# Seven block products for eight in the gate and up projections of a hybrid decoder step

## The chip, the cores and the metric

The kernel runs on one core of a Trainium2 chip. The metric is the device time of one execution in microseconds (us). The core has a matrix engine (TensorE, PE in the profile), a vector engine (VectorE, DVE), a scalar engine (ScalarE, ACT), a general engine (GpSimd, POOL) and a queue that issues the transfers (SyncE, SP).

## The reference

One layer is computed for 520 tokens, 512 of a prompt and 8 of a sample group, in float32:

```
x = x + 0.5 * swiglu(rmsnorm(x, n1), gate1, up1, down1)
h = rmsnorm(x, nm);  p = h @ w_in
     group A: x/B/C through a causal conv of width 4 and SiLU, state-space scan
              (16 heads x 64, state 128, chunks of 256), times SiLU(z), grouped norm
     group B: y = Bg * conv_w3(Cg * h_in)            (1024 channels)
x = x + concat(A, B) @ w_out
x = x + 0.5 * swiglu(rmsnorm(x, n2), gate2, up2, down2);  y = rmsnorm(x, nf)
swiglu(x) = (silu(x @ w_gate) * (x @ w_up)) @ w_down
```

The model width is 1024 (8 tiles of 128 channels), the hidden width of a half step 2816 (22 tiles), the joint projection `w_in` has 45 tiles of columns. Final states of the scan and of both convolutions are outputs too.

## The kernel before, in words

Activations lie with channels on the partitions and 520 tokens along the free axis. Every large product is made of *weight units*: up to 8 k-tiles of 128 output columns (512 KB). A unit is loaded on the SP queue and split into two parts in a reduced format whose sum is the float32 weight: ScalarE casts `hi` (L91), VectorE subtracts to get `lo` (L92). The activations are split in the same way (`xh`, `xl`). A k-tile then takes three terms, hi with xh, hi with xl and lo with xh, each for two halves of 260 tokens: six matmuls of 128x260 (`mm_k`, L118), 48 a unit. `unit` keeps one unit split ahead; `whl` has three buffers.

The stages: (1) loads of x, with the first two units cut into pieces so that products follow the loads, and GpSimd summing the squares for the norm. (2) The first half step, `ffn`: 22 times a gate unit and an up unit of 48 matmuls; VectorE takes the gate's result times the norm factor r out of PSUM (L283), ScalarE applies SiLU (L284), VectorE multiplies by r and by the up result (L285, L287) and the hidden tile is split (L290, L291). Behind all 22, the way down: 8 output tiles of 22 k-tiles (132 matmuls), each added to x by one pass (L299) and handed to `after`, which prepares the next norm. (3) The mixer: the `dt` unit, 12 conv tiles, then 24 products of the short conv during which the scan and the sample group are advanced piece by piece (`pump`), then the gate `z`, the grouped norm and the 16 units of `w_out`. (4) The second half step; its last output tile goes by token halves, each followed by the final norm of that half (`last`).

A norm factor (`factor`, L168 to L170) is a product with ones over the summed squares, a square root on ScalarE and a reciprocal on VectorE. The order of instructions on each engine comes from a scheduler that works by priorities, from the order of the code, and from estimated times; `high_priority` moves a piece forward. Tiles of one tag rotate through the buffers of their pool; a pool opened after another has closed may lie in its memory.

Of the kernel before, what the change touches and what calls it, by code (L numbers as in the profile page):

```python
# [16 lines left out]
P = 128  # L17
D = 1024
KD = D // P                  # k-tiles of the model width
SEQ = 512  # L20
NB = 8                       # sample sequences, one new token each
T = SEQ + NB                 # all tokens, prompt first
H2 = T // 2                  # tokens of one matmul
FF = 2816
KF = FF // P
NH = 16                      # SSD heads of 64 channels
HD = 64
NG = 2                       # B/C groups
NS = 128                     # state size
CW = 4                       # conv widths  # L30
SW = 3
NX = 12                      # tiles of x, B, C
NCH = SEQ // P               # blocks of 128 positions
NC2 = NCH // 2               # scan chunks of two blocks
EPS = 1e-6
KU = 8                       # k-tiles of one weight unit
WARM = 8                     # products that bring the tensor engine's clock up

# packed per-channel parameters: name -> (first column, columns)
# [15 lines left out]
def of(t):  # L55
    """k-tile k of a tile [128, k, tokens]"""
    return lambda k: t[:, k]
# [5 lines left out]

class Core:
    """The pieces that every phase uses: weight units, products, norm factors."""

    def __init__(self, nc, tc, ctx, a, order):
# [5 lines left out]
        self.wst = pool("wst", 2)  # L73
        self.whl = pool("whl", 3)
        self.nrm = pool("nrm", 2)
        self.xp = pool("xp", 1)
        self.mm = pool("mm", 3, space=space.PSUM)
        self.aux = pool("aux", 2, space=space.PSUM)
        self.dram = pool("dram", 1, space=space.DRAM)
        self.order, self.at, self.ready = order, 0, []  # L80

    # a weight unit: up to 8 k-tiles of 128 output columns, split into two float32r
    # parts whose sum is the float32 weight
    def parts(self):
        hi = self.whl.tile([P, KU, P], F32R, tag="hi", name="hi")
        lo = self.whl.tile([P, KU, P], F32R, tag="lo", name="lo")
        return hi, lo

    def split_w(self, src, st, hi, lo):
        self.nc.sync.dma_start(st, src)  # L90
        self.S.copy(hi, st)  # L91
        self.V.tensor_tensor(lo, st, hi.bitcast(F32), op=ALU.subtract)  # L92

    def fetch(self):
        if self.at == len(self.order):
            return
        src, nk, *dt = self.order[self.at]
        self.at += 1
        st = self.wst.tile([P, KU, P], F32, tag="st", name="st")
        hi, lo = self.parts()  # L100
        if any(dt):  # both parts of the few dt weights in one stationary operand
            self.nc.sync.dma_start(st, src)
            s = slice(2 * NH, 3 * NH)
            self.S.copy(hi, st)
            self.V.tensor_tensor(hi[:, :, s], st[:, :, s], hi[:, :, s].bitcast(F32), op=ALU.subtract)
        else:
            self.split_w(src, st[:, :nk], hi[:, :nk], lo[:, :nk])
        self.ready.append((hi, lo, nk))

    def unit(self, ahead=1):  # L110
        while len(self.ready) < 1 + ahead and self.at < len(self.order):
            self.fetch()
        return self.ready.pop(0)

    def mm_k(self, ps, hi, lo, k, xh, xl, first, last, hs=(0, 1)):
        for n, (w, x) in enumerate(((hi, xh), (hi, xl), (lo, xh))):
            for h in hs:
# [3 lines left out]
    def mm_unit(self, ps, u, xh, xl, first=True, last=True, hs=(0, 1)):  # L121
        hi, lo, nk = u
        for k in range(nk):
            self.mm_k(ps, hi, lo, k, xh(k), xl(k), first and k == 0, last and k == nk - 1, hs)
# [663 lines left out]
```

## Time and profile before

| | us |
|---|---|
| three runs | 1194.73, 1196.69, 1198.38 |
| median | 1196.69 |
| span of the profiled execution | 1193.0 |

For the profiled execution the span from its first to its last instruction is what is listed; the median of the runs stands 3.7 us above it, which is taken as what lies around the span. [...] Matmuls are pipelined, so the duration of one (0.28 us) is its latency; the distance between their starts is what a product costs.

### The profile page before, as it was taken

The numbers are of one execution on the slowest core, as the hardware profiler recorded it, in microseconds if no ns is written. First come the engines' busy times: TensorE is split into PE (matmuls) and PEld (weight loads), VectorE is DVE, ScalarE is ACT, GpSimd is POOL, SyncE is SP. The second block draws the span as 40 slices with busy tenths as digits, with TensorE's granted clock in tenths as the row PEclk, the third lists the DMA queues.
The fourth block names the chain that finished last, engine by engine and source line by source line (L and its number), as shares of the span: only waits on it lengthen the run. The fifth ranks groups of instructions, "written<-read, shape, count | busy, mean of one in ns | idle before, by whom it ended". The sixth has DMA issues, their size and how long they took to land.

```text
span 1193.0 us, 22147 instructions
## 1 busy us (share of the span) xinstructions
PE 1163.1 (97%) x9583; PEld 1150.2 (96%) x9583; DVE 632.9 (53%) x810; ACT 384.1 (32%) x524; POOL 254.0 (21%) x318
## 2 busy tenths in 40 slices
PE   8999999999999999998899999999999999999996
PEld 7999999999999999987889999999999999999996
DVE  7544444443333678889987476445444444432224
ACT  5322222222222466344332343223222222222221
POOL 4000000000222377567643232320000000001112
PEclk8999999999999999999999999999999999999998
DMA  5322222222332432455533222222222222232322
GB/s 197 101 96 89 89 89 92 101 87 80 98 95 89 123 107 95 144 186 166 187 107 95 78 89 91 103 90 90 89 89 92 100 93 89 90 97 81 98 81 72
DMA packets 50361, 122.99 MB, mean 103 GB/s; under 512 B 9880, under 2 KB 19256, under 8 KB 50264
## 3 DMA queue, kind: packets, MB, share of 16 engines
q1 hardware_dynamic: 50264, 121.58, 31.4%
q8 instruction: 75, 1.23, 0.4%
q14 instruction: 22, 0.18, 0.0%
HBM read 114.43 MB, written 7.14 MB: 102 GB/s over the span
## 4 chain that ended last, share of the span: by engine, by line
PE 87%; POOL 4%; DVE 4%; issue 2%; DMA 2%; ACT 1%; SPq 0%; DVEq 0%; POOLq 0%; ACTq 0%
PE mmt L118 85%; POOL st L623 1%; POOL up L622 1%; DMA out_ss<-st 1%; DMA x<-in_xT 1%; DVE lo L92 1%; DMA st<-in_ssm 1%; DVE s L561 0%; POOL t L654 0%; POOL t L653 0%; DVE s L541 0%; PE auxt L168 0%; PE mmt L403 0%; POOL xd L616 0%; DVE up L625 0%
## 5 line engine op out<-in xcount | busy, mean ns | idle before, releaser
L118 PE MATMUL mmt<-xh,hi 128*128 128x260 f32 x2112 | 429.3, 284 | 1.7 <-ACT xh L178 1.7
L118 PE MATMUL mmt<-xh,lo 128*128 128x260 f32 x2112 | 426.8, 284 | 1.0 <-DVE lo L92 1.0
L118 PE MATMUL mmt<-xl,hi 128*128 128x260 f32 x2112 | 426.8, 284 | 0.8 <-DVE xl L179 0.7
L91 ACT CAST hi<-st 128x1024 fp32r<-128x1024 f32 (+2 forms) x202 | 202.6, 1005 | 644.0 <-issue 361.7
L92 DVE TENSOR_TENSOR lo<-st,hi 128x1024 fp32r<-128x1024 f32 (+2 forms) x202 | 245.2, 1215 | 177.9 <-ACT hi L91 176.7
L118 PEld LDWEIGHTS mmt<-xh,hi 128*128 128x128 f32 x2112 | 327.1, 189 | 2.8 <-ACT xh L178 1.9
L118 PEld LDWEIGHTS mmt<-xh,lo 128*128 128x128 f32 x2112 | 326.6, 189 | 1.8 <-DVE lo L92 1.6
L118 PEld LDWEIGHTS mmt<-xl,hi 128*128 128x128 f32 x2112 | 325.8, 189 | 1.6 <-DVE xl L179 1.5
L118 PE MATMUL mmt<-hh,hi 128*128 128x260 f32 x704 | 146.5, 285 | 0.0
L118 PE MATMUL mmt<-hh,lo 128*128 128x260 f32 x704 | 145.7, 283 | 0.0
L118 PE MATMUL mmt<-hl,hi 128*128 128x260 f32 x704 | 144.5, 281 | 0.0
L143 POOL TENSOR_TENSOR acc<-x 128x520 f32<-128x520 f32 x4 | 5.4, 1349 | 560.2 <-DVE x L299 538.0
L118 PEld LDWEIGHTS mmt<-hl,hi 128*128 128x128 f32 x704 | 110.6, 189 | 0.0
L118 PEld LDWEIGHTS mmt<-hh,hi 128*128 128x128 f32 x704 | 110.5, 189 | 0.1
L118 PEld LDWEIGHTS mmt<-hh,lo 128*128 128x128 f32 x704 | 109.3, 188 | 0.0
L287 DVE TENSOR_TENSOR h<-mmt,g 128x520 f32<-128x520 f32 x44 | 30.8, 700 | 124.3 <-PE mmt L118 124.2
L283 DVE TENSOR_TENSOR g<-mmt,r 128x520 f32<-128x520 f32 x44 | 30.8, 699 | 122.9 <-PE mmt L118 122.9
L146 POOL TENSOR_TENSOR sq<-x 128x520 f32<-128x520 f32 x22 | 35.4, 1609 | 196.6 <-DVE x L299 129.8
L147 POOL TENSOR_TENSOR acc<-acc,sq 128x520 f32<-128x520 f32 x28 | 43.8, 1563 | 2.2
L179 DVE SCALAR_TENSOR_TENSOR xl<-x,pc,xh 128x520 fp32r<-128x520 f32 (+1 forms) x25 | 32.8, 1323 | 4.8 <-ACT xh L178 4.8
L285 DVE TENSOR_TENSOR g<-g,r 128x520 f32<-128x520 f32 x44 | 30.4, 694 | 1.4 <-ACT g L284 1.4
L291 DVE TENSOR_TENSOR hl<-h,hh 128x520 fp32r<-128x520 f32 x44 | 30.5, 694 | 0.7 <-ACT hh L290 0.7
(193 smaller groups left out, 1015.2 us busy)
## 6 DMA issues: line engine op xcount, KB each, us to landing
st<-in_wi SPq DMA_DIRECT2D x45, 512.0 KB, 3.5
st<-in_wg SPq DMA_DIRECT2D x43, 512.0 KB, 3.5
st<-in_wu SPq DMA_DIRECT2D x43, 512.0 KB, 3.4
st<-in_wd SPq DMA_DIRECT2D x32, 512.0 KB, 3.4
st<-in_wo SPq DMA_DIRECT2D x16, 512.0 KB, 3.6
st<-in_wd SPq DMA_DIRECT2D x16, 384.0 KB, 3.1
st<-in_ssm SPq DMA_DIRECT2D x16, 256.0 KB, 2.8
s<-scr SPq DMA_DIRECT2D x8, 512.0 KB, 4.7
```

The costliest lines, as they stand in the source:

```text
L91: self.S.copy(hi, st)
L92: self.V.tensor_tensor(lo, st, hi.bitcast(F32), op=ALU.subtract)
L118: self.PE.matmul(ps[:, h, :H2], w[:, k, :], x[:, h * H2:(h + 1) * H2], start=first and n == 0, stop=last and n == 2)
L146: eng.tensor_tensor(sq, xt, xt, op=ALU.mult)
L147: eng.tensor_tensor(acc, acc, sq, op=ALU.add)
L179: self.V.scalar_tensor_tensor(xl, xt, w, xh.bitcast(F32), op0=ALU.mult, op1=ALU.subtract)
L283: V.tensor_tensor(halves(g), pg[:, :, :H2], halves(r), op=ALU.mult)
L285: V.tensor_tensor(g, g, r, op=ALU.mult)
L287: V.tensor_tensor(halves(hf), pu[:, :, :H2], halves(g), op=ALU.mult)
L291: V.tensor_tensor(b_, hf, a_.bitcast(F32), op=ALU.subtract)
L622: G.tensor_tensor(up, bb, xd.unsqueeze(2).broadcast_to([P, HB, NS]), op=ALU.mult)
L623: G.tensor_tensor(st, st, up, op=ALU.add)
```

## The change

Gate and up no longer run as units of 128 columns but as 11 *groups* of 256 columns each. A group is a product of 2x2 blocks (columns in two tiles, tokens in two halves, channels in pairs of tiles), done with seven block products where the plain way has eight, in Winograd's form. The weights of a group come in one tile of four blocks (1 MB, `_blocks`); `adds` makes the sums of the weight blocks on VectorE, `split` splits a block pair at a time, four steps a group, four steps ahead of use (`whl` has four buffers). The activation side is made once a half step by `variants`, seven versions of 260 tokens for each pair of channel tiles. `group` accumulates the seven blocks in three PSUM banks X, Z and Y; X is read by ScalarE three times in between (`keep`), and VectorE combines the outputs (`put`, `c12`). The mixer keeps plain products (`Plain`).

The way down stays plain but is cut into four chunks of hidden pairs (`CH`), whose units are laid between later groups (`steps`), two, one, two, one and two at a time; x takes a VectorE pass of 260 tokens for each unit and half. At the end the last two output tiles go together by token halves. The squares for the norms of later stages are made by ScalarE, GpSimd only sums. In the mixer the short conv's result stays whole (`yt`) and is split into `ch` and `cl` in the gate stage. The first loads are the tiles of x, with the first weight group behind the first two. PSUM for a half step is six banks for groups and two for the rest.

```diff
-        self.wst = pool("wst", 2)
-        self.whl = pool("whl", 3)
-        self.mm = pool("mm", 3, space=space.PSUM)
+        self.raw = pool("raw", 2)
+        self.whl = pool("whl", 4)
...
+    def adds(self):
...
+                s = self.sp.tile([P, 4, 512], F32, tag="S", name="S")
+                item[3] = s
+                V = self.V
+                V.tensor_tensor(s[:, 1:3], r[:, 0:4:2], r[:, 3:4].broadcast_to([P, 2, 512]), op=ALU.add)
+                V.tensor_tensor(s[:, 0], s[:, 2], r[:, 0], op=ALU.add)
+                V.tensor_tensor(s[:, 3], r[:, 1], s[:, 0], op=ALU.add)
+                return
...
+            step = len(item) - 4
+            src = (r[:, :2], s[:, :2], s[:, 2:], r[:, 2])[step]
...
+    def block(self, ps, w, v, n, B, first, last):
+        hi, lo = (t.rearrange("p (k m) -> p k m", m=P) for t in w)
+        for k in range(n):
+            xh, xl = B(v, k)
+            for i, (a, b) in enumerate(((hi, xh), (hi, xl), (lo, xh))):
+                self.PE.matmul(ps[:, :H2], a[:, k, :], b, start=first and k + i == 0, stop=k == n - 1 and i == 2,
+                               skip_group_check=True)
+
+    def group(self, n, B, bank, ev):
+        X, Z, Y = bank(), bank(), bank()
+        of2 = lambda w, b: tuple(t[:, b] for t in w)
+        w = self.take()
+        self.block(X, of2(w, 0), 0, n, B, True, True)
+        ev.p1(X)
+        self.block(Z, of2(w, 1), 1, n, B, True, True)
+        ev.c11(Z)
+        self.split()
+        w = self.take()
+        self.block(X, of2(w, 0), 5, n, B, False, True)
+        ev.u2(X)
+        self.block(Y, of2(w, 1), 4, n, B, True, True)
+        self.split()
+        w, w4 = self.take(), self.take()
+        self.block(X, of2(w, 0), 3, n, B, False, True)
+        ev.u4(X)
+        ev.c22(Y)
+        self.block(Y, w4, 6, n, B, False, True)
+        ev.c21(Y)
+        self.split()
+        self.block(X, of2(w, 1), 2, n, B, False, True)
+        ev.c12(X)
+        self.split()
...
+    def variants(self, src, bh, bl, th, tl):
+        V, S = self.V, self.S
+        t4 = self.tv.tile([P, 4, H2], F32, tag="t4", name="t4")
+        b = src.rearrange("p m (h n) -> p (m h) n", h=2)
+        V.tensor_tensor(t4[:, :2], b[:, 0:4:3], b[:, 1:2].broadcast_to([P, 2, H2]), op=ALU.subtract)
+        S.copy(bh[:, 0], src[:, 0, T0])
+        S.copy(bh[:, 1:].rearrange("p v n -> p (v n)"), src[:, 1])
+        V.scalar_tensor_tensor(t4[:, 2], t4[:, 0], -1.0, b[:, 3], op0=ALU.mult, op1=ALU.subtract)
+        V.scalar_tensor_tensor(t4[:, 3], t4[:, 2], -1.0, b[:, 2], op0=ALU.mult, op1=ALU.subtract)
+        f = lambda t: t.rearrange("p v n -> p (v n)")
+        V.tensor_tensor(bl[:, 0], src[:, 0, T0], bh[:, 0].bitcast(F32), op=ALU.subtract)
+        V.tensor_tensor(f(bl[:, 1:]), src[:, 1], f(bh[:, 1:]).bitcast(F32), op=ALU.subtract)
+        S.copy(f(th), f(t4))
+        V.tensor_tensor(f(tl), f(t4), f(th).bitcast(F32), op=ALU.subtract)
...
+    def keep(self, ps, sign):
+        t = self.pool.tile([P, H2], F32, tag="cp", name="cp", bufs=6)
+        with self.c.tc.high_priority(400):
+            self.c.S.activation(t, ps[:, :H2], AF.Copy, scale=sign)
+        return t
...
+    def put(self, m, ts, ps, t, op):
+        with self.c.tc.high_priority(200):
+            self.c.V.tensor_tensor(self.dst[:, m, ts], t, ps[:, :H2], op=op)
...
+    def c22(self, Y):
+        self.put(1, T1, Y, self.d, ALU.subtract)
...
+        c, g, r = self.c, self.dst, self.r
+        c.V.tensor_tensor(g[:, 0, T1], X[:, :H2], r[:, T1], op=ALU.mult)
+        c.V.tensor_tensor(g[:, 0, T0], g[:, 0, T0], r[:, T0], op=ALU.mult)
+        c.V.tensor_tensor(g[:, 1], g[:, 1], r, op=ALU.mult)
+        c.S.activation(g, g, AF.Silu)
+        c.V.tensor_tensor(g, g, r.unsqueeze(1).broadcast_to([P, 2, T]), op=ALU.mult)
...
+            def prods(ps, u, i, h, hs):
...
+                V.scalar_tensor_tensor(x[h // 2][:, h % 2, hs], ps[:, :H2], 0.5, x[h // 2][:, h % 2, hs], op0=ALU.mult, op1=ALU.add)
...
-            t1 = tt.tile([P, T], F32, tag="t1", name="t1")
+            t1 = wide("t1")
...
-            S.copy(hi, t1)
-            V.tensor_tensor(lo, t1, hi.bitcast(F32), op=ALU.subtract)
...
+                S.copy(hi, yt[j])
+                V.tensor_tensor(lo, yt[j], hi.bitcast(F32), op=ALU.subtract)
```

## Rows read from the trace of the kernel before

**Rows 1.** The page: busy time of the engines, and the chain that ended last.
```profile
PE 1163.1 (97%) x9583; PEld 1150.2 (96%) x9583; DVE 632.9 (53%) x810; ACT 384.1 (32%) x524; POOL 254.0 (21%) x318
...
PE 87%; POOL 4%; DVE 4%; issue 2%; DMA 2%; ACT 1%; SPq 0%; DVEq 0%; POOLq 0%; ACTq 0%
```

**Rows 2.** Three stages: length, busy us (instructions) by engine, granted clock, DMA.
```profile
0.00:26.70 26.70, 22.12 (x126) 20.27 (x127) 20.69 (x25) 13.88 (x25) 12.35 (x13) 0.87 0.58 189
...
490.00:615.00 125.00, 110.92 (x903) 104.79 (x903) 113.09 (x173) 52.47 (x101) 85.23 (x96) 0.99 0.51 165
...
720.00:1000.00 280.00, 280.00 (x2334) 280.00 (x2333) 136.52 (x148) 80.31 (x101) 22.39 (x13) 1.00 0.27 92
```

**Rows 3.** Timeline of VectorE in gate and up: start, duration, instruction, idle before.
```profile
903.48 0.70 DVE L287 TENSOR_TENSOR h<-mmt,g 128x520 f32<-128x520 f32 x1 [3.04 <-PE mmt L118]
904.37 1.23 DVE L92 TENSOR_TENSOR lo<-st,hi 128x1024 fp32r<-128x1024 f32 x1 [0.18 <-ACT hi L91]
905.51 0.69 DVE L291 TENSOR_TENSOR hl<-h,hh 128x520 fp32r<-128x520 f32 x1
...
920.78 0.70 DVE L283 TENSOR_TENSOR g<-mmt,r 128x520 f32<-128x520 f32 x1 [3.05 <-PE mmt L118]
```

**Rows 4.** Timeline of TensorE, last output tile, first token half: first product, next thing.
```profile
1164.14 0.29 PE L118 MATMUL mmt<-hh,hi 128*128 128x260 f32 x1
...
1172.02 0.60 PE L332 MATMUL auxt<-acc,ones 128*128 128x260 f32 x2
```

**Rows 5.** Timeline of VectorE in the mixer, passes one behind the other.
```profile
476.19 2.31 DVE L497 SCALAR_TENSOR_TENSOR cv<-raw,pc,cv 128x512 f32<-128x512 f32 x3
...
481.73 1.22 DVE L560 TENSOR_TENSOR s<-s,cbm 128x1024 f32<-128x1024 f32 x1
482.86 0.68 DVE L561 TENSOR_TENSOR s<-s,cbm 128x512 f32<-128x512 f32 x1
483.46 1.22 DVE L560 TENSOR_TENSOR s<-s,cbm 128x1024 f32<-128x1024 f32 x1
```

**Rows 6.** Transfers: issues, size, median us from issue to landing.
```profile
st<-in_wg SPq DMA_DIRECT2D x43, 512.0 KB, 3.5
...
x<-in_xT SPq DMA_DIRECT2D x7, 260.0 KB, 4.3
```

**Rows 7.** Timeline of VectorE where the second half step begins.
```profile
799.25 0.70 DVE L716 TENSOR_TENSOR x<-mmt,x 128x520 f32<-128x520 f32 x1 [2.21 <-PE mmt L118]
...
808.68 3.41 DVE L170 RECIPROCAL r<-r 128x260 f32<-128x260 f32 x2
```

**Rows 8.** Timeline of VectorE in the first 24 us, two pairs of the same pass.
```profile
8.85 3.27 DVE L179 SCALAR_TENSOR_TENSOR xl<-x,pc,xh 128x520 fp32r<-128x520 f32 x2
...
19.64 1.42 DVE L179 SCALAR_TENSOR_TENSOR xl<-x,pc,xh 128x520 fp32r<-128x520 f32 x2
```

**Rows 9.** Timeline of GpSimd in the first 24 us, first and last of nine passes.
```profile
6.39 1.05 POOL L143 TENSOR_TENSOR acc<-x 128x520 f32<-128x520 f32 x1 [5.96 <-DMA x<-in_xT]
...
17.47 1.63 POOL L147 TENSOR_TENSOR acc<-acc,sq 128x520 f32<-128x520 f32 x1
```

**Rows 10.** Timeline of the end, both token halves of the last output tile.
```profile
1176.06 0.48 ACT L337 ACTIVATE rf<-auxt,eps 128x260 f32<-128x260 f32 x1 [2.95 <-PE auxt L335]
1176.57 1.78 DVE L345 RECIPROCAL rf<-rf 128x260 f32<-128x260 f32 x1 [3.53 <-ACT rf L337]
1178.38 2.96 DVE L348 TENSOR_TENSOR y<-y,rf 128x780 f32<-128x780 f32 x2
...
1181.44 0.43 DVE L309 SCALAR_TENSOR_TENSOR x<-mmt,x 128x260 f32<-128x260 f32 x1
```

**Rows 11.** Groups by line: VectorE passes of 260 from PSUM (busy us, mean ns).
```profile
L309 DVE SCALAR_TENSOR_TENSOR x<-mmt,x 128x260 f32<-128x260 f32 x2 | 0.9, 428 | 6.4 <-PE mmt L118 6.3
```

**Rows 12.** Timeline of TensorE in the first 35 us, order of the first products.
```profile
9.57 1.07 PE L118 MATMUL mmt<-xh,hi 128*128 128x260 f32 x4
10.70 0.80 PE L118 MATMUL mmt<-xl,hi 128*128 128x260 f32 x2
```

## What was predicted, ahead of the result

> **What bounds the kernel now.** The page's engine totals come first: TensorE is busy for 97% of the span, VectorE for 53%, and TensorE holds 87% of the chain that ended last [rows 1]. The stages say where that is not so [rows 2]. From 720 to 1000 us (gate and up of the second half step) TensorE is busy all the time and VectorE for 136.5 of 280 us. In the mixer's stage from 490 to 615 us TensorE stands for 14 us and VectorE is busy 113.1 of 125, a share of 0.905. The first 26.7 us hold 126 matmuls. So the half steps are set by the number of matmuls, the mixer's middle by VectorE, and the start by loads and operand preparation.
>
> The VectorE timeline of a half step gives the cadence: three units of 48 matmuls lie between 903.48 and 920.78, that is 17.30 / 144 = 0.1201 us a matmul [rows 3]. In these units VectorE has waits of 3 us and more.
>
> **The matmuls removed.** A group (a 256-column pair of gate or up) was 2 units of 48 matmuls and becomes 7 blocks of 4 k-tiles by 3 terms, 84. There are 11 pairs, gate and up, two half steps: 44 groups, 528 matmuls fewer, 528 x 0.1201 = **-63.4 us**. A block's 12 matmuls now write one bank in a row, where the two token halves alternated. The last channel tile of before already does that, 66 matmuls from 1164.14 to 1172.02, 0.119 each [rows 4]; so the cadence is not at risk. The way down keeps its 1056 matmuls a half step.
>
> **What a group costs VectorE.** Back to back, a pass of 1024 elements starts 1.13 us before its successor, one of 512 takes 0.60 [rows 5], so 260, 520 and 1040 come to 0.33, 0.61 and 1.16 by that slope. Two short passes that wait for each other cost more: 2.31 / 3 = 0.77 for 512 with a per-channel scalar in the same rows, about 0.68 without. A group then takes: splitting 7 blocks of 512 (3 x 1.13 + 0.60 = 4.0), the block sums (1.13 + 2 x 0.68 = 2.5), three reads of a bank by `put` (1.0), and `c12` with its last pass of 1040 (0.33 + 0.33 + 0.61 + 1.16 = 2.4): **10.0 us** of VectorE beside 84 x 0.1201 = 10.1 of TensorE. That is the heart of the matter. VectorE goes from half busy to fully busy wherever groups stand alone. A unit of the way down brings 36 matmuls (4.3 us) and costs VectorE about 1.6 (a 768 split and two passes of 260), so with it TensorE leads again. By `steps`, six groups come before the first unit; later only the up groups of pairs 5, 8 and 10 stand alone. So I cost the first six groups of each half step by VectorE, at the 0.905 that it reached in rows 2.
>
> **First half step.** VectorE can begin when both tiles of x pair 0 are there: issue near 1.65, 4.3 to land [rows 6], 0.7 for ScalarE's scaling (taken as a VectorE pass of 520), 6.7 us. Until group 5 is out it has `variants` four times (0.61, two dependent 0.43, 0.34, 0.61, 1.16: 3.6 each, 14.3), the two reciprocals of the norm factor (3.4, as at 808.68 [rows 7]), sums and splits of six groups and a quarter of the seventh (6.25 x 6.5 = 40.8) and six evacuations (6 x 3.43 = 20.6): 79.1. GpSimd squares and sums meanwhile: a pair of 520 passes took 3.27 beside it and 1.42 after it, 0.92 lost a pass [rows 8]; GpSimd ran without a pause up to 19.1 [rows 9]. The change leaves it ten such passes; I take 8 us. (79.1 + 8) / 0.905 + 6.7 = 102.9. TensorE has then done 504 matmuls and about 30 of group 6, 64.1 us, so 38.8 are lost. Before, 102 products (126 less 16 warm-ups and 8 for the factor), 12.3 us, came out of 26.7: 14.4 lost. Difference **+24**. Bounds: no gaps and no contention, 85.8, +7; every pass at its whole duration (a group 11.05, factor 1.105) and 10.5 of contention, +36. I take the share that a saturated stage showed.
>
> [...]
>
> **Second half step.** Before, nothing was lost at the entry; the last evacuation at 799.25 [rows 7] fell behind products of seven ready k-tiles. Now the block sums wait for a pool opened after the mixer's closes, so for its last product. VectorE then has 0.7 for the evacuation, 3.0 left of `variants`, 3.4 for the reciprocals, 40.8 and 20.6: 68.5, over 0.905 is 75.7 against 64.1 of TensorE, **+11**. Bounds +4 (no gaps) and +19 (whole durations).
>
> **The other 32 groups.** X and Y are read and accumulated again. X is read by ScalarE while one block of 12 matmuls (1.44 us) covers it: free. Y is not so covered: block 6 must wait until `c22` has read it, and that needs ScalarE's copy of X, made after block 3, directly in front. A copy is 0.48 [rows 10], the VectorE pass 0.43 [rows 11], and each may stand behind a pass of a microsecond: 0.9 to 2.2 us in each group unless other products are put there. The scheduler does put them: at 9.57 four hi products of both units stand together, out of the order of the code [rows 12]. Units of the way down and the next group's first blocks (other banks, weights split three units ahead) are candidates. I take 0.2 a group, **+6**; bounds 0 and 1.2 (38).
>
> **Tail and mixer.** At the end the two token halves are 24 matmuls (2.9 us) apart; before, they were 66 matmuls (7.9 us by rows 4) and the norm's products apart, so the first half's reciprocal and y passes (1.78 and 2.96) were done by 1181.34, just ahead of the second evacuation [rows 10]. Now they collide with it: 0 to 4.7, I take **+3**. Splitting y of the short conv into `ch`, `cl` leaves the saturated stage for the gate stage, eight passes of 0.61: 0 to -5, I take **-3**. Loads: the same bytes; a group's 1 MB, twice 3.5 us at most by the 512 KB rows [rows 6], has some 10 us. ScalarE's three copies and a wider Silu fit beside its 80.3 busy of 280 [rows 2]: nothing.
>
> **Sum.** -63.4 + 24 + 11 + 6 + 3 - 3 = -22.4 on a span of 1193.0: 1170.6; the median of the runs lies 3.7 above that span, so **1174**. All lower bounds give 1139, all upper ones 1232.
>
> **Rivals.** *VectorE keeps ahead*: the start near its lower bound, gaps all filled, 1139 to 1158. For it: weights wait four deep, and half the VectorE work hangs on no product. Against it: the first six groups have no other product to fill with. 0.22.
>
> *Passes do not overlap*: when each waits on another engine, a group costs VectorE 11.05: start +34, entry +19, the rest as above, 1192. Against it: the overlap in rows 3 (904.37 to 905.51, with 1.23 us long); for it, most passes of 260 hang on a bank just finished. 0.13. [...]
>
> *The wait for Y in every group*: PE's order leaves `c22` uncovered. -63.4 + 24 + 11 + 3 - 3 = -28.4 is eaten at 0.89 us a group; at 1.5, 32 groups cost 48 and the time is 1216, slower. For it: nothing lies between in the code, and `bank` gives only six banks, three to a group. Against it: the reordering above. 0.13.
>
> Forecast (1158 to 1190): 0.50; 0.02 for others.
>
> **Numbers.** Range 1146 to 1200: it cuts part of the first rival and nearly all of the last. Faster by over 0.3% (3.6 us, about what these runs can tell from no change): 0.22 + 0.50 + half of the second rival, 0.79. Within: 0.08. Slower: 0.13.
>
> **What would show it.** Product matmuls 528 fewer at 0.120. VectorE above 0.85 busy up to 100 us and for some 75 us behind the mixer, TensorE with gaps there, and full from then on; the sixth group out near 103 us. In the later groups idle TensorE before block 6, released by `put`, under 0.3 us a group. At the start the granted clock (a mean of 0.87 in the first stretch of rows 2) stays at its lower level for longer, hidden behind VectorE's work. The prediction is wrong if TensorE is full from 40 us on (too slow a forecast), if a group takes 12 us or more in the middle (too fast), or if the cadence leaves 0.120.

## The result, and the profile after

The changed kernel takes 1182.72 us (median of four runs, 1180.01 to 1185.23) against 1196.95 for the kernel before (four runs on the same chip): ratio 0.9883, 95% interval 0.986 to 0.9906. It is 1.2% faster. The forecast was 1174, so it promised 22.7 us and 14.2 came. The profiled execution took 1180.4, its span is 1178.6.

First the page of the changed kernel, busy time by engine and the chain that ended last; they answer to [rows 1].

```profile
PE 1117.5 (95%) x9059; PEld 1095.7 (93%) x9059; DVE 897.8 (76%) x1305; ACT 523.5 (44%) x750; POOL 227.1 (19%) x302
...
PE 79%; DVE 8%; POOL 5%; issue 3%; DMA 2%; ACT 2%; DVEq 0%; SPq 0%; POOLq 0%; ACTq 0%
```

There are 524 matmuls fewer, VectorE goes from 53% to 76%, and TensorE's share of the chain falls from 87% to 79%: what was saved there has partly come back as waits. Where, the stretches tell. Columns: stretch, its length, busy us (instructions) of PE, its weight loads, DVE, ACT and POOL, then the granted clock as a share of full speed, and the transfers.

```profile
0.00:26.70 26.70, 12.08 (x37) 8.82 (x37) 21.48 (x22) 15.70 (x24) 15.52 (x14) 0.67 0.49 165
490.00:615.00 125.00, 109.23 (x862) 103.12 (x863) 108.86 (x170) 49.44 (x95) 84.29 (x95) 0.95 0.50 163
720.00:1000.00 280.00, 272.86 (x2243) 270.90 (x2242) 210.02 (x284) 122.44 (x170) 11.73 (x8) 0.99 0.27 91
...
20.00:40.00 20.00, 11.57 (x37) 8.93 (x38) 19.77 (x26) 11.53 (x19) 3.86 (x2) 0.59 0.15 52
60.00:80.00 20.00, 20.00 (x167) 19.92 (x166) 19.35 (x28) 12.00 (x17) 0.00 (x0) 1.00 0.31 106
80.00:100.00 20.00, 20.00 (x167) 19.80 (x166) 19.53 (x29) 11.21 (x17) 0.00 (x0) 1.00 0.22 73
...
800.00:810.00 10.00, 7.56 (x52) 6.66 (x52) 9.93 (x12) 7.20 (x11) 1.73 (x1) 1.00 0.05 7
810.00:820.00 10.00, 5.49 (x32) 5.20 (x32) 8.45 (x10) 1.43 (x2) 0.00 (x0) 0.66 0.25 99
820.00:840.00 20.00, 20.00 (x167) 19.85 (x167) 17.32 (x26) 11.93 (x18) 0.00 (x0) 1.00 0.29 106
```

The reader is to see three things. The first three stretches are those of [rows 2]: 37 matmuls for 126 in the first 26.7 us, and 862 for 903 in the mixer's middle. Between 60 and 100 us VectorE is busy for 38.9 of 40 us and TensorE still has no gap: it is busy all 40 us. And at the entry of the second half step, 800 to 820, 84 matmuls stand where a full stretch has 167.

The start in detail, on VectorE: `vbl` and `vtl` (L258 to L261) are the operands that `variants` makes, `S` (L132 to L134) the block sums, L288 the reciprocals of the norm factor.

```profile
6.54 1.50 DVE L258 TENSOR_TENSOR vbl<-xw,vbh 128x260 fp32r<-128x260 f32 x1
...
10.39 2.07 DVE L132 TENSOR_TENSOR S<-raw 128x1024 f32<-128x1024 f32 x1
12.38 2.32 DVE L261 TENSOR_TENSOR vtl<-t,vth 128x1040 fp32r<-128x1040 f32 x1
...
25.07 1.21 DVE L132 TENSOR_TENSOR S<-raw 128x1024 f32<-128x1024 f32 x1
26.21 2.31 DVE L261 TENSOR_TENSOR vtl<-t,vth 128x1040 fp32r<-128x1040 f32 x1
...
31.55 1.76 DVE L288 RECIPROCAL r<-r 128x260 f32<-128x260 f32 x1
33.24 0.36 DVE L256 SCALAR_TENSOR_TENSOR t<-t,xw 128x260 f32<-128x260 f32 x1
33.52 1.76 DVE L288 RECIPROCAL r<-r 128x260 f32<-128x260 f32 x1
35.20 1.17 DVE L261 TENSOR_TENSOR vtl<-t,vth 128x1040 fp32r<-128x1040 f32 x1
...
40.83 1.23 DVE L261 TENSOR_TENSOR vtl<-t,vth 128x1040 fp32r<-128x1040 f32 x1
```

Every block runs over all four channel pairs. Blocks 0 to 2 take `vb` operands alone, and the first two were complete when VectorE read them out at 38.89; the other four take `vt` operands, and none of them is complete before the last `vtl`, which starts at 40.83. Ahead of it stand the second group's sums (25.07) and both reciprocals, which nothing needs yet, and some passes of the first 27 us have durations far over their own: 1.50 for 260 elements, which take 0.42 elsewhere, and 2.32 for 1040, which take 1.23. TensorE's last wait of this part ends at 53.51.

The entry of the second half step, TensorE's waits, then VectorE:

```profile
801.60 0.36 PE L211 MATMUL pst<-vbh,hi 128*128 128x260 f32 x1 [1.78 <-DVE x L991]
...
814.60 0.59 PE L211 MATMUL pst<-vtl,hi 128*128 128x260 f32 x1 [4.51 <-DVE vtl L261]
```

```profile
799.62 1.22 DVE L132 TENSOR_TENSOR S<-raw 128x1024 f32<-128x1024 f32 x1 [1.81 <-PE mmt L195]
800.76 0.69 DVE L991 TENSOR_TENSOR x<-mmt,x 128x520 f32<-128x520 f32 x1
...
808.59 3.40 DVE L288 RECIPROCAL r<-r 128x260 f32<-128x260 f32 x2
811.91 1.16 DVE L132 TENSOR_TENSOR S<-raw 128x1024 f32<-128x1024 f32 x1
812.99 0.41 DVE L380 TENSOR_TENSOR g<-cp,pst 128x260 f32<-128x260 f32 x1
813.32 1.23 DVE L261 TENSOR_TENSOR vtl<-t,vth 128x1040 fp32r<-128x1040 f32 x1
```

Both waits are a matter of order. A block sum runs ahead of the residual add (L991) that the last operands hang on, which is 1.1 of the 1.78 us, and the reciprocals and the second group's first sum run ahead of the last `vtl`, for which TensorE waits 4.51 us.

At the end of the kernel, VectorE again; it answers to [rows 10].

```profile
1162.30 1.78 DVE L601 RECIPROCAL rf<-rf 128x260 f32<-128x260 f32 x1 [0.57 <-ACT rf L592]
1164.00 0.36 DVE L523 SCALAR_TENSOR_TENSOR x<-auxt,x 128x260 f32<-128x260 f32 x1
1164.28 2.94 DVE L604 TENSOR_TENSOR y<-y,rf 128x780 f32<-128x780 f32 x2
1167.14 0.34 DVE L594 TENSOR_SCALAR y<-x,pc 128x260 f32<-128x260 f32 x1
```

The first token half's reciprocal and y passes now stand among the second half's passes: from the start of the last product (1162.92) to the end of the span are 15.7 us, where before they were 11.9.

**Accounts.** With a product at 0.1201 us (831 matmuls in 100 us from 200 on: 0.1203) the span divides so. All stretches are taken from the start of one stage's last product to the start of the next one's. The first half step's last product starts at 391.45 instead of 394.92, with 26 products of the mixer (3.1 us) already done: 6.6 us earlier, where the matmuls removed give 31.7, so **25.1** are lost. The mixer, from there to its last product, takes 411.2 with these 26 counted, for 404.0: **7.2** lost. The second half step takes 363.4 for 382.2, 18.8 less instead of 31.7: **12.9** lost. The tail loses **3.8**. Together -63.4 + 25.1 + 7.2 + 12.9 + 3.8 = -14.4, the difference of the spans.

### The profile page after: what moved, and what is told of

Same layout as the page of the kernel before. It is cut to its first block, busy times and chain, and to the rows that moved or that the text cites. A ratio compares the mean times of both kernels' runs of the same rounds, so it can differ in the third digit from the quotient of the medians.

```text
span 1178.6 us, 21684 instructions
## 1 busy us (share of the span) xinstructions
PE 1117.5 (95%) x9059; PEld 1095.7 (93%) x9059; DVE 897.8 (76%) x1305; ACT 523.5 (44%) x750; POOL 227.1 (19%) x302
## 4 chain that ended last, share of the span: by engine, by line
PE 79%; DVE 8%; POOL 5%; issue 3%; DMA 2%; ACT 2%; DVEq 0%; SPq 0%; POOLq 0%; ACTq 0%
PE pst L211 37%; PE auxt L522 21%; PE mmt L195 20%; DVE lo L147 2%; POOL up L891 1%; POOL st L892 1%; DVE r L288 1%; ACT hi L146 1%; DMA raw<-in_wu 1%; DMA out_ss<-st 1%; DMA st<-in_ssm 1%; DVE S L132 1%; DVE cv L766 1%; DVE vtl L261 0%; DVE y L604 0%
## 5 line engine op out<-in xcount | busy, mean ns | idle before, releaser
L146 ACT CAST hi<-raw 128x1024 fp32r<-128x1024 f32 (+2 forms) x212 | 185.8, 878 | 269.5 <-PE pst L211 86.3
L147 DVE TENSOR_TENSOR lo<-raw,hi 128x1024 fp32r<-128x1024 f32 (+2 forms) x212 | 220.3, 1040 | 50.0 <-ACT hi L146 47.3
L211 PE MATMUL pst<-vtl,hi 128*128 128x260 f32 x704 | 199.4, 284 | 6.8 <-DVE vtl L261 6.8
L211 PE MATMUL pst<-vth,hi 128*128 128x260 f32 x704 | 199.4, 285 | 4.2 <-ACT vth L260 3.5
L522 PE MATMUL auxt<-hh,hi 128*128 128x260 f32 x704 | 197.7, 283 | 1.1 <-DVE x L523 0.7
L522 PE MATMUL auxt<-hl,hi 128*128 128x260 f32 x704 | 197.6, 283 | 0.0
L211 PE MATMUL pst<-vth,lo 128*128 128x260 f32 x704 | 196.9, 284 | 0.2 <-DVE lo L147 0.2
L522 PE MATMUL auxt<-hh,lo 128*128 128x260 f32 x704 | 194.5, 283 | 0.0
L211 PE MATMUL pst<-vbh,hi 128*128 128x260 f32 x528 | 150.6, 289 | 10.7 <-ACT hi L146 5.1
L211 PE MATMUL pst<-vbl,hi 128*128 128x260 f32 x528 | 150.0, 287 | 5.1 <-DVE vbl L258 4.0
```

The costliest lines, as they stand in the source:

```text
L146: self.S.copy(hi, src)
L147: self.V.tensor_tensor(lo, src, hi.bitcast(F32), op=ALU.subtract)
L211: self.PE.matmul(ps[:, :H2], a[:, k, :], b, start=first and k + i == 0, stop=k == n - 1 and i == 2, skip_group_check=True)
L522: PE.matmul(ps[:, :H2], w[:, k, :], v, start=k + n == 0, stop=k == nk - 1 and n == 2)
```

## The experiments

Two theories were set against each other. **A**, the prediction's: the first six groups of a half step run at VectorE's pace, so the loss follows from all the work VectorE has up to the sixth group. **B**, from the profile after: the loss lies wholly ahead of the last operand, and what counts is what stands in that chain. All edits below are to the changed kernel, and times of the changed kernel that they are set against are its 1182.72. Its four runs lie in two pairs, 1180.0 and 1180.4, 1185.0 and 1185.2, so a difference from their median of less than some 3 us is not clear of the spread. Matmul counts and waits are read from one profiled execution of each kernel.

| run | median us | ratio to before, 95% interval |
|---|---|---|
| block sums left out | 1172.80 | 0.9793 (0.9777 to 0.981) |
| block sums twice | 1271.04 | 1.0614 (1.0578 to 1.0651) |
| first sum twice | 1215.79 | 1.0153 (1.0137 to 1.0169) |
| reciprocals behind the last operand | 1179.40 | 0.9852 (0.9835 to 0.9869) |
| and the sums | 1179.83 | 0.9863 (0.9846 to 0.9879) |
| and a buffer for each pair | 1178.72 | 0.9846 (0.9823 to 0.9869) |
| and squares without GpSimd | 1168.78 | 0.9766 (0.975 to 0.9781) |
| and the same at the entry | 1169.46 | 0.9763 (0.974 to 0.9785) |
| squares without GpSimd alone | 1178.05 | 0.9836 (0.9822 to 0.985) |
| three banks | 1180.11 | 0.9862 (0.9849 to 0.9875) |
| way down not spread | 1195.44 | 0.9981 (0.9972 to 0.9991) |
| split put back in the mixer | 1182.08 | 0.9876 (0.9858 to 0.9894) |

**Block sums left out.**

```diff
-                s = self.sp.tile([P, 4, 512], F32, tag="S", name="S")
...
-                V.tensor_tensor(s[:, 3], r[:, 1], s[:, 0], op=ALU.add)
+                item[3] = r
```

> Left out: the four weight sums of each gate or up group (their products take the loaded blocks instead, so the result is not the reference's); VectorE has 2.6 us a group less, every product stays. Theory A (the prediction's: the first six groups of each half step run at VectorE's pace, so the loss is a matter of how much VectorE has to do by the sixth group): six groups less 2.6 us at a busy share of 0.905, 17 us in the first half step and up to the whole 13 us of its loss in the second, about 1155 us. Theory B (the loss lies ahead of the first block products, in what VectorE does before the last operand of the block products is there; from 53 us on TensorE is full): only the sums that stand ahead of that operand count, 6.9 us in the first half step and 3.7 in the second, about 1172 us, with TensorE full from about 47 us on.

1172.8, 9.9 us less: theory B. By 60 us TensorE has 234 matmuls for 213 (2.5 us), and in the 25 us behind the mixer's last product 181 for 124 (6.8 us); that makes 9.3. In the middle nothing changes, though VectorE's load falls by a fifth: 200 to 300 us holds 831 matmuls with the sums and 831 without. B's detail of the first half step was wrong, however. Full stretches begin at 51 us and not at the 47 expected, because the last `vtl` came only 2.1 us earlier (38.70): freed of the sums, VectorE waited ahead of it for ScalarE's casts (2.2 us in all), and its passes beside GpSimd were still long (an operand subtract at 16.15 took 2.31).

**Sums twice, and the first sum twice.** Dose against response.

```diff
+                for _ in range(2):
+                    V.tensor_tensor(s[:, 1:3], r[:, 0:4:2], r[:, 3:4].broadcast_to([P, 2, 512]), op=ALU.add)
+                    V.tensor_tensor(s[:, 0], s[:, 2], r[:, 0], op=ALU.add)
+                    V.tensor_tensor(s[:, 3], r[:, 1], s[:, 0], op=ALU.add)
```

> Every weight sum is computed twice into the same place (result unchanged); VectorE has 2.6 us a group more, 12.6 us against TensorE's 10.1. If VectorE is at its rate limit in the first six groups of a half step, as its busy share of 0.97 between 60 and 100 us says: 7 + 15 us in the first half step and 4 + 15 in the second, TensorE with gaps until about 120 us, some 1220 us. If VectorE has room there and only what stands ahead of the last operand counts: 7 + 4, some 1194 us.

1271.0, 88.3 us more, and both theories are far off. The loss isn't at the front but everywhere. Columns as above, the kernel with the sums twice:

```profile
60.00:100.00 40.00, 35.80 (x278) 34.76 (x277) 36.76 (x52) 19.30 (x27) 0.00 (x0) 0.96 0.22 80
200.00:300.00 100.00, 92.25 (x740) 90.51 (x739) 81.72 (x120) 37.69 (x53) 0.00 (x0) 0.98 0.24 81
900.00:1000.00 100.00, 90.80 (x695) 89.38 (x696) 87.70 (x125) 42.21 (x58) 0.00 (x0) 0.93 0.23 77
```

VectorE isn't full there: 82 of 100 us, and TensorE still falls to 740 matmuls from 831. What VectorE waits for from 120 to 390 us (us in total, times, longest):

```profile
DVE S L133 <- DMA raw<-in_wu: 19.2, 8, 3.5
DVE lo L148 <- ACT hi L147: 13.3, 9, 3.4
DVE h L381 <- ACT cp L367: 7.2, 3, 3.5
DVE x L524 <- PE auxt L523: 5.8, 5, 1.9
DVE S L133 <- DMA raw<-in_wg: 5.0, 2, 4.0
```

The first adds of a group wait 24 us for loads, more than for anything else. A load needs one of two buffers (`raw`), and a buffer comes free with the last split of its blocks, which stands behind the sums: load, sums, splits, next load make a ring in which the added work counts whole. That ring is argued from these rows and the code, not shown: no run has a third buffer, and the sums themselves have only one buffer (`sp`), which would make a ring of the same kind.

```diff
                 V.tensor_tensor(s[:, 1:3], r[:, 0:4:2], r[:, 3:4].broadcast_to([P, 2, 512]), op=ALU.add)
+                V.tensor_tensor(s[:, 1:3], r[:, 0:4:2], r[:, 3:4].broadcast_to([P, 2, 512]), op=ALU.add)
```

> Only the first of the three weight sums (128x1024, 1.22 us) is computed twice in each gate or up group, result unchanged. All sums twice cost 88 us, 2.0 us for each of the 44 groups and in every part of both half steps, for 2.6 us of added work. If the chain from a load to the last subtract of a group has a margin of about 0.6 us behind which everything counts: 0.6 us times 44, some 1211 us. If there is no margin: 54 us more, some 1236 us. If only the first six groups of a half step are bound by VectorE (the prediction): 12 x 1.2, some 1197 us.

1215.8, 33.1 us more: 0.75 us for each of the 44 groups where 1.22 were added, 2.01 where 2.6 were. Between the two doses 1.38 us of work cost 1.26. So a group has, on average, a margin of some 0.5 to 0.6 us (1.22 less 0.75, 2.6 less 2.01), and what goes beyond it counts almost whole. The average hides an uneven spread: with the first sum twice, 5.6 of the 33.1 us are lost by 60 us (166 matmuls for 213), the 100 us from 200 on lose 2.2 (813 for 831), those from 900 on 4.8 (794 for 834). The estimate by a margin (1211) came nearest; the prediction's (the first six groups alone) would have been 1197.

**Order on VectorE.** First only the reciprocals, then the sums too: each is queued behind an earlier instruction of VectorE, with the same work: the reciprocals and the second group's sums behind the half step's last `vtl`, the first group's sums at the entry behind the last residual add.

```diff
-                self.V.reciprocal(r[:, hs], r[:, hs])
+                with self.behind(behind):
+                    self.V.reciprocal(r[:, hs], r[:, hs])
```

> The four reciprocals of the norm factors in front of the two half steps are issued behind the last operand subtract on VectorE instead of ahead of it (same work). Theory B: the last operand is 3.5 us earlier in each half step, and so is the first full stretch of TensorE: 7 us less than the changed kernel, some 1176 us; the wait for that operand at 809.9 falls from 4.5 us to about 1. Theory A: the same work has been done by the sixth group, no change (within 2 us).

1179.4, 3.3 us less instead of 7, and the intervals of the two ratios still touch. At the entry it works as expected: 154 matmuls in the 25 us behind the mixer's last product for 124, 3.6 us. At the start it doesn't: the last `vtl` comes at 39.21, 1.6 us earlier, and 216 matmuls for 213 by 60 us. The reciprocals had stood beside a chain that was itself waiting: the kernel makes the operands of one channel pair after the other in one buffer, scaling, differences, cast on ScalarE, subtract, and only then the next pair.

```diff
+                with self.behind(self.sums_behind):
+                    V.tensor_tensor(s[:, 1:3], r[:, 0:4:2], r[:, 3:4].broadcast_to([P, 2, 512]), op=ALU.add)
```

> As the run with the reciprocals behind the last operand; besides, the weight sums of the second group stand behind that operand too, and at the entry of the second half step the sums of the first group stand behind the last residual add (same work, only VectorE's order). Theory B: another 2.6 us in the first half step, 1.2 and 1.2 in the second, some 1171 us; TensorE's first wait at the entry (1.8 us for the residual add) is gone. Theory A: no change against the changed kernel (within 2 us).

1179.83: no gain in time over the run before, though its rows move. The last `vtl` is at 35.72, TensorE has 239 matmuls by 60 us, 26 more than the changed kernel (3.1 us), and 149 in the 25 us of the entry, 25 more than the changed kernel but 5 fewer than with the reciprocals alone. By these 6 us were due and 2.9 came; its four runs spread from 1175.6 to 1182.2, and the run can't settle that term.

**A buffer for each pair, and the squares.**

```diff
-        t4 = self.tv.tile([P, 4, H2], F32, tag="t4", name="t4")
+        t4 = (hp or self.tv).tile([P, 4, H2], F32, tag="hl" if hp else "t4", name="t4")
...
-        xw = c.tv.tile([P, 2, T], F32, tag="xw", name="xw")
+        xw = (hp or c.tv).tile([P, 2, T], F32, tag="hh" if hp else "xw", name="xw")
```

`hp` is the pool of the hidden tiles, which lies empty at the start of the first half step.

> As the run with VectorE's order changed; besides, the scaled input and the four differences of the first half step get a buffer of their own for each of the four channel pairs, so that a pair needn't wait for the subtract of the pair before. There the last operand came at 36.9 us, with VectorE idle for 2.8 us ahead of it on ScalarE's casts and GpSimd squares slowing it. If the single buffers hold it up: last operand at about 33 us, 2 to 3 us less than that run, some 1177 us; if VectorE's own work does: no change.

1178.72, with a last `vtl` at 35.09 and 249 matmuls by 60 us: 1.2 us more work done than in the run before, and no difference in time that six runs from 1172.4 to 1183.5 show. Buffers on top of the order were not it. Its trace shows what was, first GpSimd, then ScalarE:

```profile
21.08 8.71 POOL L287 TENSOR_TENSOR acc<-acc,sq 128x520 f32<-128x520 f32 x1 [3.72 <-ACT sq L284]
```

```profile
29.83 0.64 ACT L284 ACTIVATE sq<-x 128x520 f32<-128x520 f32 x1 [7.03 <-POOL acc L287]
```

One GpSimd pass lasted 8.71 us, while VectorE ran one pass behind the other up to 28.66. ScalarE's next square needs the one buffer that this pass reads, so ScalarE stood for 7.03 us with the casts of `vth` queued behind that square, and VectorE then waited 2.79 us for such a cast.

```diff
-                        if e < 2:
-                            c.square(acc[0], x[e][:, m], e + m == 0)
...
+                    S.activation(sq, x[e], AF.Square)
+                    for h in range(2):
+                        for m in range(2):
+                            PE.matmul(pq[h][:, :H2], c.ones, sq[:, m, h * H2:(h + 1) * H2], start=e + m == 0, stop=e + m == NQ)
```

> As the run with a buffer for each pair; besides, the squares of the first half step are taken by ScalarE and summed over tiles by TensorE's products with ones (16 of 0.64 us while it has nothing else), so that GpSimd does nothing there. The operand work of VectorE in the first 20 us of the changed kernel has instructions of 1.2 to 2.3 us that elsewhere take 0.4 to 1.2; 6.6 us in sum. If GpSimd beside it is the cause: the same instructions at 0.42, 0.69 and 1.2 us, last operand at about 28 us, 4 to 6 us less than the run with a buffer for each pair, some 1172 us. If it is not: the same long durations and no change.

**1168.78**, 9.9 us less than the run with the buffers and 13.9 less than the changed kernel: the fastest version, 2.3% under the kernel before. VectorE in its first 26 us (here L142 is the sum, L268 to L271 the operands):

```profile
6.24 0.42 DVE L268 TENSOR_TENSOR vbl<-xw,vbh 128x260 fp32r<-128x260 f32 x1
...
8.82 1.23 DVE L142 TENSOR_TENSOR S<-raw 128x1024 f32<-128x1024 f32 x1 [0.72 <-DMA raw<-in_wg]
...
11.10 1.24 DVE L271 TENSOR_TENSOR vtl<-t,vth 128x1040 fp32r<-128x1040 f32 x1
...
24.20 2.38 DVE L271 TENSOR_TENSOR vtl<-t,vth 128x1040 fp32r<-128x1040 f32 x2
```

The passes that took 1.50, 2.07 and 2.32 take 0.42, 1.23 and 1.24. The last `vtl` is done at 26.6 instead of 42, TensorE's last wait ends at 31.81 instead of 53.51, and by 60 us it has 346 matmuls for 213, of which 8 are more products with ones: 125 x 0.12 = 15 us. Of these 12.5 are left at the half step's last add (379.33 for 391.86). The entry wins 25 matmuls, 3.0 us, and gives most of them back in the groups: 2493 matmuls from 822 to 1125 us for 2511, with 2.1 us of waits for casts and adds where the changed kernel has 0.3. That fits the groups' small margin, met earlier; no run tests it.

Which of the three edits did it? The squares alone (the last diff), with the old order and the single buffers:

> The changed kernel with one alteration: the squares of the first half step are taken by ScalarE and summed by TensorE, GpSimd does nothing there; the order on VectorE and the single buffers stay. If GpSimd beside VectorE is what the 14 us between the changed kernel and the run with order, buffers and squares altered come from: first full stretch of TensorE about 10 us earlier than 53.5, some 1172 us. If the single buffers hold each pair's operands up until the pair before is done: the 6.6 us of long instructions are saved and no more, some 1177 us.

1178.05, 4.7 us less, TensorE's last wait at 47.96, 284 matmuls by 60 us. So the 13.9 are not GpSimd's alone, and by the run with the buffers they are not those of order and buffers alone. With the order and the buffers but GpSimd busy, 36 products were won by 60 us (4.3 us); with GpSimd quiet but the old order and one buffer, 63 (7.6 us, of which 4.7 show between the medians and 1.4 between the two traced spans, 1177.2 and 1178.6); with all three 125 (15 us). The links stood one behind the other: VectorE's long passes, ScalarE held by the buffer of the squares, and the old order with its single buffers. Whether the order or the buffers are needed beside the squares was not separated: no run has the squares with only one of the two.

At the entry, the squares of the last pair alone:

```diff
-        for m in range(2):
+        for m in range(2 if e < NQ - 1 else 0):
             c.square(self.acc, self.x[e][:, m], e + m == 0, True)
...
+                for h in range(2):
+                    c.PE.matmul(pq[h][:, :H2], c.ones, sq[:, h * H2:(h + 1) * H2], start=False, stop=m == 1)
```

> As the run with order, buffers and squares of the first half step altered; besides, at the entry of the second half step the squares of the last channel pair are summed by TensorE instead of GpSimd. There one sum on VectorE took 1.80 us where it takes 0.68 elsewhere, and one subtract 1.33 for 0.42. If GpSimd is the cause: both short, 1 to 2 us less than that run, some 1167 us; if not, no change.

1169.46: no change. The passes did shorten, the sum from 1.80 to 0.69 and the subtract from 1.33 to 0.43, but 156 matmuls for 149 in its 25 us are 0.8 us.

**Three banks.**

```diff
-            pp = pool("pp", 6, space=bass.MemoryType.PSUM)
+            pp = pool("pp", 3, space=bass.MemoryType.PSUM)
```

> Three PSUM banks instead of six for the block groups (same work). If what hides the evacuations inside a group (block 6 waits for c22 from Y) is that TensorE starts the next group or a block of the way down in other banks: without them the next group waits for the last evacuations of X and Y, 0.4 to 1.5 us for each of the 44 groups, 18 to 66 us more, some 1200 to 1249 us. If the evacuations are quick enough by themselves (put issued ahead, 0.42 us): no more than 6 us, the term of the prediction.

1180.11: no loss at all. What TensorE waited for from 60 to 390 us, in all:

```profile
PE pst L211 <- DVE lo L147: 0.6, 2, 0.3
PE pst L211 <- ACT cp L366: 0.5, 2, 0.2
PE auxt L522 <- DVE x L523: 0.4, 1, 0.4
```

1.5 us in nearly the whole first half step. The order of its instructions tells why three are enough, though the trace doesn't name the banks: Z is read out early, so the next group's block 0 goes into Z's bank and stands between blocks 2 and 6 of this group, and where the way down is due its products stand there. By that order the wait for Y has its cover in either case; my expectation, that the cover needs three more banks, fell.

**Way down not spread.**

```diff
-SPREAD = (2, 1, 2, 1, 2)
+SPREAD = (8,)
```

> The eight blocks of a chunk of the way down come all behind one block group instead of two, one, two, one and two behind five groups (same work). If a group by itself keeps TensorE full, as the six groups in front of the first chunk do from 53 to 120 us: within 3 us of the changed kernel, some 1183 us. If the groups need the blocks of the way down between them, because a group's VectorE and load chain is as long as its products: the groups without blocks lose 0.5 to 2 us each, 30 groups in all, some 1198 to 1240 us.

1195.44, 12.7 us more, so the way the chunks are laid is most of the gain. But the place is neither theory's. Elsewhere the half step runs full (829 matmuls from 200 to 300). What is lost is lost where a half step runs out, first in this kernel, then in the changed one:

```profile
360.00:380.00 20.00, 17.18 (x118) 16.68 (x117) 12.74 (x22) 9.47 (x15) 1.11 (x2) 0.83 0.28 79
...
369.97 0.80 PE L522 MATMUL auxt<-hh,hi 128*128 128x260 f32 x2 [2.34 <-ACT hh L547]
```

```profile
360.00:380.00 20.00, 19.57 (x164) 19.40 (x163) 13.28 (x24) 10.49 (x18) 4.74 (x4) 1.00 0.39 110
```

The last pair's hidden tile has to be multiplied, cast and split before its way down can begin. Spread, the third chunk's last units are still there to fill that time; in one lump they have been used up (read from the code). The wait is 2.3 us, and behind it the matmuls stand 0.217 us apart up to 376.6, then 0.120 again; the granted clock of the 20 us is 0.83. (In the kernel before, 0.217 is their distance from 13.46 to 14.33, and the granted clock from 10 to 15 us is 0.50.) That makes 46 matmuls fewer, 5.5 us, and 36 fewer from 1140 to 1160.

**The split put back in the mixer.**

```diff
             yt.append(y)
+            S.copy(t1, y)
+            V.tensor_tensor(t1, y, t1, op=ALU.subtract)
```

> In each of the mixer's eight short convolutions a ScalarE copy and a VectorE subtract of 128x520 are put back (their result is used by nothing, the output is unchanged), as the kernel before had them there; the later ones stay. The prediction's step (VectorE is full between 490 and 600 us, so eight subtracts less there are 3 us less): 3 to 6 us more than the changed kernel, some 1187 us. The rival (VectorE waits there in its order for the sample loop's GpSimd additions and for loads, 12 us idle at five places between 550 and 600): within 1.5 us of the changed kernel.

1182.08: eight more subtracts on VectorE cost nothing that the runs show. In the stretch of [rows 2] they even bring back the order of before: VectorE's waits at 569.92 and 597.30 are those of the kernel before at 570.25 and 597.63.

```profile
490.00:615.00 125.00, 110.91 (x898) 104.40 (x896) 112.54 (x173) 52.73 (x101) 84.66 (x95) 0.97 0.51 164
```

898 matmuls for 862 in the changed kernel (903 before), though VectorE does more. The stretch hangs on a chain of short pieces, and on where in the queue each engine finds them. In the changed kernel VectorE stood still in it for the sample group's additions on GpSimd (L892) and for a load of the scan (`scr`):

```profile
560.30 0.69 DVE L894 TENSOR_TENSOR up<-st,cc 128x512 f32<-128x512 f32 x1 [1.35 <-POOL st L892]
577.47 0.88 DVE L810 TENSOR_SCALAR s<-s,acs 128x128 f32<-128x128 f32 x4 [3.53 <-DMA s<-scr]
591.15 0.69 DVE L894 TENSOR_TENSOR up<-st,cc 128x512 f32<-128x512 f32 x1 [1.38 <-POOL st L892]
```

The 36 matmuls won there are lost at other places of the same run: 748 from 395.21 to 490 for 767, with a wait of 2.0 us for the norm factor's table load (1.28 us long, at 404.14 in the changed kernel) that the changed kernel has too (1.5) and the kernel before hadn't. Which of the mixer's changes puts that wait there was not tried.

## Why the prediction was right, and by how much it missed

The direction, the range and the main sum held: 528 products at 0.120 us, less a start, less an entry, less a tail. That the total came within 8.4 us is in part luck: the term for the groups was too high by 6 and the mixer's too low by 10. Point by point, predicted and measured:

- **Matmuls removed, -63.4:** as predicted; the cadence stayed.
- **First half step, +24; 25.1.** The size is right, the step behind it is not, and so the agreement is in part luck. "I cost the first six groups of each half step by VectorE, at the 0.905" spread the loss over 100 us. VectorE ran at 0.97 from 60 to 100 us beside a TensorE without gaps, and all was lost before 53.5, where the prediction had expected gaps up to 100. The amount of VectorE's work up to the sixth group was about right: VectorE is busy for 88.4 of the first 100 us, and 543 matmuls by 100 us less 24 of warm-up and norm are 6.2 groups, so the sixth was out a little ahead of the 103 us forecast. But a sum over the work of an engine doesn't say what can be done about it. Theory A promised up to 30 us from leaving the sums out, and 9.9 came; winning 14 us took no work away from the kernel, only another order, buffers, and the squares moved off GpSimd. The 10.5 us of contention in the term's upper bound are shown by no run: nine passes beside GpSimd lost 8.7. (In the recorded sum 6.25 x 6.5 is 40.6, and by `steps` the up group of pair 10 has a unit behind it; neither changes the forecast.)
- **Second half step, +11; 12.9.** The terms (reciprocals, sums, last operands) were those that the rows show, but as two waits in the first 15 us behind the mixer, not as gaps over six groups. TensorE is full from 820 on.
- **Other groups, wait for Y, +6; 0.** The run with three banks shows the cover, the next group's block 0 or the way down.
- **Tail, +3; 3.8.** As predicted, by the rows of the end: the first half's passes stand among the second's. No run changes that order.
- **Mixer, -3; +7.2.** This is the step that failed: "eight passes of 0.61" taken out of "the saturated stage". A busy share of 0.905 was read as a bound. Putting the subtracts back cost nothing, so leaving them out had not been worth anything; TensorE lost 41 matmuls (4.9 us) in that stretch by another order of the same pieces and 18 (2.2 us) ahead of it. That the removal of work changed the order in that stretch is shown by the run with the split put back; why the whole mixer stayed 6 us slower than before even in that run is open.
- **Around the span, +3.7; 4.1** (1182.7 less 1178.6). The reading behind it was wrong: a run's time is 1.8 us above its own span (1180.4 and 1178.6). The rest of both numbers is that each profiled execution was faster than the median.

The mixer's 10.2 and the entry's 1.9 too little, the groups' 6 too much, and 2.3 in small terms make the 8.4 us between 1174.3 and 1182.7.

Of the rivals, *VectorE keeps ahead* was half right: gaps in the groups were all filled, but the start was at its middle value, not near its lower bound. *Passes do not overlap* fell: the subtract at 9.25 has its successor at 10.39, 1.14 later, though it is 1.21 long. *The wait for Y in every group* fell by the three banks. But the doubled sums show how near it was to one like it: some 0.5 us more work in a group would have begun to cost, and at 1.22 us more the change was slower than the kernel before, 1215.8.

## What to carry to other kernels

When a change trades matmuls for vector work, compare the engines' totals to see whether it can pay, but look for the loss in the chain that stands before the last operand of the first products: what runs there ahead of its need, in one buffer, or beside an engine that slows it. Ask of the steady part not how full the vector engine is but how long the ring of buffers around it may be (load, sums, splits, buffer free), and find its margin by adding a known dose. And a stage at 0.9 busy isn't bound by that engine until taking work away, or putting it back, moves the time.

## What the runs showed of the hardware

VectorE passes with two inputs in SBUF took longer beside GpSimd passes: in the changed kernel 1.50 (at 6.54) and 2.32 (at 12.38), where the run without GpSimd's squares shows 0.42 and 1.24, 1.08 more each time. A GpSimd pass beside an idle VectorE took 1.05 there (4.00 to 5.05). Seven passes of the first 20 us lost 6.6 us in sum, four of them some 1.08 each and three 0.5 to 0.9; with two more, at 23.38 and 26.21, it was 8.7, where the prediction took 8 and counted them as so much work.

GpSimd was slower as well: in the run with a buffer for each pair one of its passes lasted 8.71 us (21.08 to 29.79) and ended 1.13 us behind the last of a row of VectorE passes. Where order and buffers had been loosened first, taking the squares off GpSimd gave 9.9 us of time; what in it is VectorE's shorter passes and what is ScalarE's 7.03 us of waiting was not separated.

The record of the granted clock is not to be taken alone. In the first 40 us it says 0.72 and 0.59 (0 to 20 and 20 to 40 us) for the changed kernel and 1.00 in both for the kernel with three banks, whose start is the same. But the matmuls stand equally far apart in both, 0.217 us instead of the 0.120 that the changed kernel shows at a granted clock of 1.00 (831 in the 100 us from 200 on): at 36.67, 36.89 and 37.10 in the changed kernel, and in the other

```profile
36.73 0.42 PE L211 MATMUL pst<-vtl,hi 128*128 128x260 f32 x1
36.95 0.42 PE L211 MATMUL pst<-vth,lo 128*128 128x260 f32 x1
```

By that distance both ran equally slowly there; the changed kernel's granted clock from 36.5 to 38 us is 0.50.
